# A hybrid SSD and attention layer: the projections of the next head are placed three steps ahead from the first step, and the lead shrinks by one step per head

## The chip, the core and the metric

One core of a Trainium2 chip runs the whole layer in one launch. The metric is the time of that launch in microseconds on the device. TensorE (PE) multiplies, VectorE (DVE), ScalarE (ACT) and GpSimd (POOL) do the element-wise work, SyncE (SP) issues most of the loads. Each engine works through its own instructions in the order in which they stand; semaphores make one engine wait for another.

## The reference

The layer normalises `x` (1024 tokens, 1024 wide), projects it once, and splits the columns between a Mamba-2 scan and a differential attention; both results go through an output projection, and a gated MLP follows. The change concerns the attention alone: 8 heads, each with two query and two key maps of 64 and a value of 128, queries and keys normalised and partly rotated, a mask by chunks of 64 keys.

```
q, k = rope(rms_norm(q)), rope(rms_norm(k))            # per head, 2 maps of 64
sc = einsum("bhjqd,bhjkd->bhjqk", q_blk, kt) * scale   # q_blk: 128 queries
p = softmax(where(mask, sc, -inf)); w = p[:, :, 0] - lam * p[:, :, 1]
o = einsum("bhqk,bhkv->bhqv", w, vt)
o = rms_norm(o, subln_w) * (1 - lambda_init)
```

## The kernel before

**Stages.** A start computes the normalised input, the whole projection of head 0 and the first three tiles of head 1. Then a loop of 64 steps runs the attention; step n is head h = n // 8 and place i = n % 8, which takes query tile `QORDER[i]` (0, 4, 1, 7, 2, 6, 3, 5; tile qt sees (qt + 1) x 128 keys). Scan, output projection and MLP follow; PE has little idle time there.

**One step.** The letters of `STEP = "SPWAB"` (line 37) are traced in this order: S, `softmax` of the next step's query tile (two score tiles `ps_s` in PSUM, one per map; DVE takes the maximum, ACT the exponential `pt`, DVE joins the two maps); P, `project`; W, `w_transpose` of this step's weights (`ps_wt` on PE, `wt` out on ACT or DVE); A, `values` of the step before (`po`; after each fourth tile `att_norm` squares the four results `ob` on ACT, and `att_store` transposes them, `ps_ot`); B, `build_qk` (`ps_qt` on PE, four casts `qka` on ACT, four subtractions on DVE, two copies on POOL).

**A projection tile.** `proj_mm(h, t)` is 24 matmuls of 384 columns (lines 209 to 211) into one `ps_pj`; `proj_post` (line 308) reads it with three ACT operations (`sq`, `raw`, `v`), two on DVE, and eight on POOL. `PROJ_AT[i]` (line 48) gives the tiles of head h + 1 that step i projects, `BUILD_AT[i]` those that it builds. Tiles 0 to 2 of head 1 were projected in the start, so steps 0 to 2 have none. Every head has one step with two tiles (place 5) and one with none (place 7); a step with no tile is called free below. When tile 7 is traced, the weights of the head after are loaded: `load_piece` casts the high part `wh` on ACT and subtracts on POOL or DVE. Two of the four pieces have a buffer for one head only, so their casts wait for the last matmuls of tile 7.

**What sets the order.** A scheduler lays the traced instructions out per engine and gives out the buffers; on the chip that order is fixed. PSUM has 3 slots `mm` (for `ps_pj`, `ps_qt`, `ps_wt`, `ps_ot`, `ps_tr`), 2 slots `s` (for `ps_s`, one per map, so one step's pair fills them) and one `o` (for `po`). A score matmul waits until the exponential of the map that held its slot is done.

Of the kernel before, what the change touches and what calls it, by code (L numbers as in the profile page):

```python
# [7 lines left out]
F32 = mybir.dt.float32  # L8
# [7 lines left out]
P = 128  # L16
S = 1024
NT = S // P
DK = 1024 // P
NH = 8  # L20
# [16 lines left out]
STEP = "SPWAB"  # L37
LAG = 1
WV = 1
RAW = 5  # L40
KT = 5
RS = 1

# [1 line left out]
START = "q0 w2 w3 q12 w1 q3 q4 q56 b0 b1 b3 w0 a0 a1 c1 c0 b2 b4 S0 p7 a2 r1 q7 b7 r0 c2 b5 b6 r2"  # L45
QORDER = [0, 4, 1, 7, 2, 6, 3, 5]

PROJ_AT = [[0], [1], [2], [3], [4], [5, 6], [7], []]
BUILD_AT = [[], [], [0], [1, 2], [3], [4], [5, 6], [7]]


PK_N1 = 0
# [22 lines left out]
def layer(ctx, tc, xT, wq0, wqkv, wxz, wout, wgu, wdn, pk, pb, cst, rot, sel, out):  # L75
# [137 lines left out]
    def proj_mm(h, t):  # L213
        ps = psa.tile([P, 512], F32, tag="mm", name="ps_pj")
        for k in KORDER:
            proj_k(h, t, k, ps)
        return ps
# [4 lines left out]
    ap_ = pool(actx, "att", side="right")  # L222
# [46 lines left out]
    for k in range(DK):  # L269
# [4 lines left out]
        n = 512 if k == 0 else S  # L274
# [22 lines left out]
    q0p = pool(a1ctx, "qk0")  # L297
# [10 lines left out]
    def proj_post(h, ts, pss_):  # L308
        hd = heads[h]
        n = len(ts)  # L310
        raws = []
        fac = ap_.tile([P, 2, 4], F32, tag="fac", name="fac", bufs=3)[:, :n]
        for i, (t, ps) in enumerate(zip(ts, pss_)):
            sq = a1.tile([P, 256], F32, tag="sq", name="sq", bufs=1)
            A.activation(sq, ps[:, 0:256], AF.Square)
            raw = a1.tile([P, 4, 64], F32, tag="raw", name="raw", bufs=RAW)
            raws.append(raw)
            q4 = raw.rearrange("p (i j) d -> p i j d", j=2)
            if h < WV:
                V.tensor_tensor(out=q4, in0=ps[:, 0:256].rearrange("p (i j d) -> p i j d", j=2, d=64), in1=b4(w_qk), op=ALU.mult)  # L320
            else:
                A.copy(out=raw.rearrange("p g d -> p (g d)"), in_=ps[:, 0:256])
                G.tensor_tensor(out=q4[:, :, :, 16:64], in0=q4[:, :, :, 16:64], in1=b4(w_qk[:, :, 16:64]), op=ALU.mult)
            v = (q0p, ap_)[h % 2].tile([P, P], F32, tag="v", name="v", bufs=8)
            A.activation(v, ps[:, 256:384], AF.Copy, scale=rtok[:, t : t + 1])
            hd["v"][t] = v
            if h == 0:
                V.tensor_scalar(out=dtt[:, t, :], in0=ps[:, 384:400], scalar1=rtok[:, t : t + 1], scalar2=None, op0=ALU.mult)
            V.tensor_reduce(out=fac[:, i], in_=sq.rearrange("p (g d) -> p g d", d=64), axis=AX.X, op=ALU.add)
            (V if h == 0 else G).tensor_scalar(out=fac[:, i], in0=fac[:, i], scalar1=1.0 / 64.0, scalar2=eps2[:, t : t + 1], op0=ALU.mult, op1=ALU.add)  # L330
            ta = a1.tile([P, 4, 16], F32, tag="ra", name="ra", bufs=2)
            tb = a1.tile([P, 4, 16], F32, tag="rb", name="rb", bufs=2)
            ta4 = ta.rearrange("p (i j) d -> p i j d", j=2)
            tb4 = tb.rearrange("p (i j) d -> p i j d", j=2)
            G.tensor_tensor(out=ta4, in0=q4[:, :, :, 0:16], in1=b4(cw[:, t]), op=ALU.mult)
            G.tensor_tensor(out=tb4[:, :, :, 0:8], in0=q4[:, :, :, 8:16], in1=b4(sw[:, t, :, 0:8]), op=ALU.mult)
            G.tensor_tensor(out=tb4[:, :, :, 8:16], in0=q4[:, :, :, 0:8], in1=b4(sw[:, t, :, 8:16]), op=ALU.mult)
            G.tensor_tensor(out=raw[:, :, 0:16], in0=ta, in1=tb, op=ALU.add)
        G.tensor_tensor(out=fac, in0=fac, in1=mhalf.unsqueeze(2).broadcast_to([P, n, 4]), op=ALU.pow)
        for i, t in enumerate(ts):  # L340
            V.tensor_tensor(out=raws[i], in0=raws[i], in1=fac[:, i].unsqueeze(2).broadcast_to([P, 4, 64]), op=ALU.mult)
            hd["qk"][t] = raws[i]
# [103 lines left out]
    class Piece:  # L446
        n = 0
# [121 lines left out]
    for op in START.split():  # L569
        t = int(op[1])  # L570
# [39 lines left out]

        return get

    def project(h, i):
        if h + 1 < NH:
            for t in PROJ_AT[i]:
                if h > 0 or t > 2:
                    proj_post(h + 1, [t], [proj_mm(h + 1, t)])
            if NT - 1 in PROJ_AT[i] and h + 2 < NH:
                for c in (2, 3, 0, 1):
                    load_piece(h + 2, c)  # L620
        else:
            half()
            if i == 2:
                dt_rates()
            if i == 4:
                dt_decays()
# [15 lines left out]
    for n, (h, i) in enumerate(steps):  # L642
        for part in STEP:
            if part == "S" and n + 1 < len(steps):
                h2, i2 = steps[n + 1]
                sm[n + 1] = softmax(h2, QORDER[i2])
            elif part == "P":
                project(h, i)
            elif part == "W":
                w, rl = sm.pop(n)  # L650
                todo[n] = (w, rl, w_transpose(QORDER[i], w))
            elif part == "B":
                for t in BUILD_AT[i]:
                    if h + 1 < NH:
                        build_qk(h + 1, t)
            elif part == "A":
                if n >= LAG:
                    values(n - LAG)
# [379 lines left out]
    for d in range(DK):  # L1038
        t = xq.tile([P, S], F32, name=f"x2_{d}")
# [443 lines left out]
```

## Time and profile before

| | |
|---|---|
| median of 3 runs | 1674.99 us (1673.95 to 1675.69) |
| profiled execution | 1673.81 us, its span 1672.0 us |
| PE busy | 1620.7 us, 97% of the span |
| DVE, ACT, POOL busy | 1138.0, 785.8, 776.2 us |
| the chain that ended last | PE 79%, DVE 9%, DMA 3%, ACT 3%, issue 3%, POOL 2% |
| step 0 begins, step 7 of head 0 begins | about 69 us, about 120 us |

Busy time of PE counts modelled ends of matmuls, so a busy PE need not be at its peak. In a timeline row the time in brackets is the idle time of the engine just before, with what ended it. From the first start to the next start of an instruction is what it takes in a row of work; a mean duration contains an overlap with the next.

### The profile page before, as it was taken

Reading aid. Unit: us, or ns where it says so; the run is one execution under the profiler, and the core shown is the slowest. Engines: PE = TensorE matmul, PEld = TensorE weight load, DVE = VectorE, ACT = ScalarE, POOL = GpSimd, SP = SyncE. Lnnn points to the kernel's source line nnn. Section 1 sums busy time; section 2 is a strip of 40 time slices with the busy share of each in tenths; the row PEclk is TensorE's granted clock in tenths of the full one; section 3 lists DMA queues with packets and bytes.
Section 4 is the critical chain, followed back from the end, with each engine's and each line's share of the span. In section 5 each row is a group of like instructions: output and inputs, shape, how many; then the busy total and the mean of one; then the engine's idle time right before and its main releaser. Section 6 shows DMA issues by size and latency. Waiting matters only on the chain.

```text
span 1672.0 us, 23812 instructions
## 1 busy us (share of the span) xinstructions
PE 1620.7 (97%) x8237; PEld 1378.3 (82%) x8237; DVE 1138.0 (68%) x2096; ACT 785.8 (47%) x1759; POOL 776.2 (46%) x975
## 2 busy tenths in 40 slices
PE   7899999999999999999999998899999999999998
PEld 7799999999988877877778876688888888777887
DVE  7778777777787667876752258855555555789877
ACT  5566675766666454445532234333333222534431
POOL 5856766675541232243324337733444443343225
PEclk9899999999999999999999999999999999999999
DMA  5101110110011110131325321432233222755523
GB/s 189 38 17 36 51 36 17 52 45 14 21 58 38 51 39 32 45 133 45 114 68 192 115 92 39 132 107 99 103 103 112 95 101 89 250 191 175 166 93 113
DMA packets 78135, 146.49 MB, mean 88 GB/s; under 512 B 8490, under 2 KB 16938, under 8 KB 78016
## 3 DMA queue, kind: packets, MB, share of 16 engines
q1 hardware_dynamic: 65216, 129.38, 23.1%
q0 software_dynamic: 2864, 10.10, 1.7%
q10 hardware_dynamic: 9936, 5.51, 1.1%
q8 instruction: 65, 1.06, 0.3%
q14 instruction: 54, 0.44, 0.1%
HBM read 110.09 MB, written 34.87 MB: 87 GB/s over the span
## 4 chain that ended last, share of the span: by engine, by line
PE 79%; DVE 9%; DMA 3%; ACT 3%; issue 3%; POOL 2%; SPq 0%; DVEq 0%; ACTq 0%; POOLq 0%
PE ps_pj L211 5%; PE ps_pj L209 5%; PE ps_pj L210 5%; PE ps_x L485 4%; PE ps_x L486 4%; PE ps_x L487 4%; PE ps_c L170 3%; PE ps_c L171 3%; PE ps_c L172 3%; PE ps_d L172 3%; PE ps_d L171 3%; PE ps_d L170 3%; PE ps_a L170 3%; PE p L172 3%; PE ps_a L171 3%; PE ps_a L172 3%
## 5 line engine op out<-in xcount | busy, mean ns | idle before, releaser
L158 ACT CAST op<-wr 128x512 fp32r<-128x512 f32 x156 | 96.2, 619 | 260.2 <-PE ps_d L172 77.7
L159 DVE TENSOR_TENSOR op<-wr,op 128x512 fp32r<-128x512 f32 x108 | 88.4, 820 | 146.4 <-ACT op L158 135.8
L1174 POOL TENSOR_TENSOR t<-wr,t 128x512 f32<-128x512 f32 (+2 forms) x72 | 93.6, 1299 | 193.9 <-issue 123.8
L209 PE MATMUL ps_pj<-wh,xwh 128*128 128x384 f32 (+1 forms) x512 | 175.7, 347 | 5.9 <-ACT wh L152 5.9
L211 PE MATMUL ps_pj<-wh,xwl 128*128 128x384 f32 (+1 forms) x512 | 174.0, 342 | 3.8 <-DVE xwl L278 3.8
L210 PE MATMUL ps_pj<-wl,xwh 128*128 128x384 f32 (+1 forms) x512 | 174.6, 342 | 0.0
L159 POOL TENSOR_TENSOR op<-wr,op 128x512 fp32r<-128x512 f32 x48 | 65.1, 1356 | 214.2 <-ACT op L158 213.9
L1174 POOL TENSOR_TENSOR t<-wr 128x512 f32<-128x512 f32 (+2 forms) x72 | 89.3, 1242 | 104.4 <-DVE op L159 33.6
L485 PE MATMUL ps_x<-xwh,op 128*128 128x512 f32 x320 | 130.3, 407 | 0.3 <-DVE raw L509 0.3
L486 PE MATMUL ps_x<-xwl,op 128*128 128x512 f32 x320 | 127.1, 397 | 0.0
L487 PE MATMUL ps_x<-xwh,op 128*128 128x512 f32 x320 | 127.1, 397 | 0.0
L382 ACT ACTIVATE pt<-ps_s,nm 128x640 f32<-128x640 f32 (+7 forms) x128 | 94.4, 740 | 47.3 <-DVE nm L377 20.0
L209 PEld LDWEIGHTS ps_pj<-wh,xwh 128*128 128x128 f32 x512 | 97.7, 191 | 6.5 <-ACT wh L152 5.9
L158 ACT CAST op<-t 128x512 fp32r<-128x512 f32 x80 | 49.5, 621 | 112.1 <-PE ps_c L172 55.6
L211 PEld LDWEIGHTS ps_pj<-wh,xwl 128*128 128x128 f32 x512 | 97.6, 191 | 4.9 <-DVE xwl L278 4.8
L171 PE MATMUL p<-y,op 128*128 128x512 f32 x256 | 100.8, 396 | 0.0
L172 PE MATMUL p<-y,op 128*128 128x512 f32 x256 | 100.6, 396 | 0.0
L170 PE MATMUL p<-y,op 128*128 128x512 f32 x256 | 99.0, 398 | 0.0
L159 DVE TENSOR_TENSOR op<-t,op 128x512 fp32r<-128x512 f32 x80 | 77.1, 966 | 32.0 <-ACT op L158 31.3
L210 PEld LDWEIGHTS ps_pj<-wl,xwh 128*128 128x128 f32 x512 | 97.7, 191 | 0.4
L377 DVE TENSOR_REDUCE nm<-ps_s 128x1 f32<-128x640 f32 (+7 forms) x128 | 94.0, 746 | 1.7
L410 PE MATMUL po<-v,wt 128*128 128x128 f32 x576 | 77.4, 276 | 0.3 <-DVE ob L420 0.3
(302 smaller groups left out, 4650.9 us busy)
## 6 DMA issues: line engine op xcount, KB each, us to landing
wr<-in_wgu_dram SPq DMA_DIRECT2D x88, 256.0 KB, 2.8
mr<-md SPq DMA_DIRECT2D x77, 256.0 KB, 3.7
wr<-in_wout_dram SPq DMA_DIRECT2D x48, 256.0 KB, 2.7
wr<-in_wqkv_dram SPq DMA_DIRECT2D x28, 384.0 KB, 3.1
wr<-in_wxz_dram SPq DMA_DIRECT2D x40, 256.0 KB, 2.8
wr<-in_wdn_dram SPq DMA_DIRECT2D x12, 768.0 KB, 4.8
md<-m SPq DMA_DIRECT2D x30, 256.0 KB, 2.0
big<-yd SPq DMA_DIRECT2D x10, 512.0 KB, 4.0
```

The costliest lines, as they stand in the source:

```text
L158: A.copy(out=op[:, 0:n], in_=src)
L159: eng.tensor_tensor(out=op[:, n : 2 * n], in0=src, in1=op[:, 0:n], op=ALU.subtract)
L170: T.matmul(out=ps, lhsT=wh, rhs=a[:, 0:512], start=first, stop=False, skip_group_check=more)
L171: T.matmul(out=ps, lhsT=wh, rhs=a[:, 512:1024], start=False, stop=False, skip_group_check=more)
L172: T.matmul(out=ps, lhsT=wl, rhs=a[:, 0:512], start=False, stop=last, skip_group_check=more)
L209: T.matmul(out=ps[:, :n], lhsT=xwh[k][:, ts], rhs=wh[:, k % 2, :], start=k == first, stop=False)
L210: T.matmul(out=ps[:, :n], lhsT=xwh[k][:, ts], rhs=wl[:, k % 2, :], start=False, stop=False)
L211: T.matmul(out=ps[:, :n], lhsT=xwl[k][:, ts], rhs=wh[:, k % 2, :], start=False, stop=k == last)
L485: T.matmul(out=ps, lhsT=wh[:, ks], rhs=xwh[k][:, fs], start=k == 0, stop=False)
L486: T.matmul(out=ps, lhsT=wh[:, ks], rhs=xwl[k][:, fs], start=False, stop=False)
L487: T.matmul(out=ps, lhsT=wl[:, ks], rhs=xwh[k][:, fs], start=False, stop=k == DK - 1)
L1174: G.tensor_tensor(out=self.t[name], in0=x, in1=y, op=ALU.subtract)
```

## The change

The two tables now hold, for each head, the step number n of each tile. Head 1: tiles 3 to 7 are projected in steps 0 to 4 (before in 3, 4, 5, 5, 6). Head 2: steps 6 to 13 (before 8 to 14, two of them in 13). Head 3: steps 15 to 22 (before 16 to 22, two of them in 21). Heads 4 to 7 keep their places. The builds follow: head 1 in steps 0 to 6, head 2 in 8 to 14, head 3 in 17 to 23. So the free steps up to step 23 are 5, 14 and 23 (before 0, 1, 2, 7, 15 and 23), and no step before 24 has two tiles. Six `raw` buffers (before 5) and 10 and 9 `v` buffers (before 8 each) hold what is made early; they cost memory alone.

```diff
-RAW = 5
+RAW = 6
...
-PROJ_AT = [[0], [1], [2], [3], [4], [5, 6], [7], []]
-BUILD_AT = [[], [], [0], [1, 2], [3], [4], [5, 6], [7]]
+PROJ_AT = {h: [9 * h - 12 + t for t in range(8)] if h < 4 else [8 * h - 8 + t - t // 6 for t in range(8)] for h in range(1, 8)}
+BUILD_AT = {h: [9 * h - 9 + (0, 1, 1, 2, 3, 4, 5, 6)[t] - (h > 1) for t in range(8)] if h < 4 else [8 * h - 8 + (2, 3, 3, 4, 5, 6, 6, 7)[t] for t in range(8)] for h in range(1, 8)}
+def at_step(table, n):
+    return [(h, t) for h, row in table.items() for t, m in enumerate(row) if m == n]
...
-            v = (q0p, ap_)[h % 2].tile([P, P], F32, tag="v", name="v", bufs=8)
+            v = (q0p, ap_)[h % 2].tile([P, P], F32, tag="v", name="v", bufs=(10, 9)[h % 2])
...
-    def project(h, i):
-        if h + 1 < NH:
-            for t in PROJ_AT[i]:
-                if h > 0 or t > 2:
-                    proj_post(h + 1, [t], [proj_mm(h + 1, t)])
-            if NT - 1 in PROJ_AT[i] and h + 2 < NH:
+    def project(n):
+        h, i = steps[n]
+        for h1, t in at_step(PROJ_AT, n):
+            proj_post(h1, [t], [proj_mm(h1, t)])
+            if t == NT - 1 and h1 + 1 < NH:
                 for c in (2, 3, 0, 1):
-                    load_piece(h + 2, c)
-        else:
+                    load_piece(h1 + 1, c)
+        if h == NH - 1:
             half()
...
-                project(h, i)
+                project(n)
...
-                for t in BUILD_AT[i]:
-                    if h + 1 < NH:
-                        build_qk(h + 1, t)
+                for h1, t in at_step(BUILD_AT, n):
+                    build_qk(h1, t)
```

On PE, at the start of the loop before (tiles numbered by the program: `ps_qt_797`, `_840` and `_853` build head 0; `ps_s_954` is a map of query tile 7; `ps_wt_909` and `ps_wt_939` are weights of steps 0 and 1):

```order
L350 MATMUL ps_qt_797<-cst_sb_60,raw_782 128x128 x2
L350 MATMUL ps_qt_840<-cst_sb_60,raw_550 128x128 x2
L372 MATMUL ps_s_954<-qka0_437 128x512
L373 MATMUL ps_s_954<-klo0_439,qka0_437 128x512
L350 MATMUL ps_qt_853<-cst_sb_60,raw_565 128x128 x2
L398 MATMUL ps_wt_909<-cst_sb_60,pt_712 128x128
L121 MATMUL ps_tr_914<-cst_sb_60,wide_67 40x128
L372 MATMUL ps_s_954<-qka0_437 128x512
L398 MATMUL ps_wt_939<-cst_sb_60,pt_898 128x128 x4
```

And now (`ps_s_1079` is the same map of query tile 7, `ps_pj_909` tile 3 of head 1, of which the first and last of 24 rows are shown, `ps_wt_952` the weights of step 0):

```order
L358 MATMUL ps_qt_797<-cst_sb_60,raw_782 128x128 x2
L358 MATMUL ps_qt_840<-cst_sb_60,raw_550 128x128 x2
L358 MATMUL ps_qt_853<-cst_sb_60,raw_565 128x128 x2
L380 MATMUL ps_s_1079<-qka0_437 128x512
L381 MATMUL ps_s_1079<-klo0_439,qka0_437 128x512
L217 MATMUL ps_pj_909<-wh_460,xwh4_102 128x384
...
L219 MATMUL ps_pj_909<-wh_506,xwl3_109 128x384
L406 MATMUL ps_wt_952<-cst_sb_60,pt_712 128x128
L358 MATMUL ps_qt_956<-cst_sb_60,raw_813 128x128 x2
L380 MATMUL ps_s_1079<-qka0_437 128x512
L381 MATMUL ps_s_1079<-klo0_439,qka0_437 128x512
L129 MATMUL ps_tr_970<-cst_sb_60,wide_67 40x128
```

A whole projection tile has come behind the first two scores of query tile 7, and the third build of head 0 ahead of them.

On PE, the free step at the end of head 0 before, from the last matmul of head 1's projections (`ps_pj_1386`) to the first of head 2's (`ps_pj_1568`); `ps_s_1495` and `_1496` are the maps of head 1's query tile 0, `ps_s_1545` and `_1546` those of tile 4:

```order
L211 MATMUL ps_pj_1386<-wh_506,xwl3_109 128x384
L398 MATMUL ps_wt_1453<-cst_sb_60,pt_1223 128x128 x4
...
L410 MATMUL po_1333<-v_567,wt_1331 128x128
L350 MATMUL ps_qt_1467<-cst_sb_60,raw_1262 128x128 x2
L372 MATMUL ps_s_1495<-qka1_438 128x128
...
L372 MATMUL ps_s_1496<-qka1_438 128x128
...
L350 MATMUL ps_qt_1480<-cst_sb_60,raw_1305 128x128 x2
L398 MATMUL ps_wt_1514<-cst_sb_60,pt_1375 128x128 x4
...
L372 MATMUL ps_s_1545<-qka1_438 128x512
...
L372 MATMUL ps_s_1546<-qka1_438 128x512
...
L350 MATMUL ps_qt_1530<-cst_sb_60,raw_1414 128x128 x2
L209 MATMUL ps_pj_1568<-wh_1430,xwh4_102 128x384
```

The stretch between the same two projections now, in step 5 (`ps_pj_1286` to `ps_pj_1479`); `ps_s_1395` is the second map of query tile 3, `ps_s_1456` and `_1457` those of tile 5, `ps_s_1551` the first map of head 1's tile 0, `ps_ot_1430` the first transposed result of head 0:

```order
L219 MATMUL ps_pj_1286<-wh_506,xwl3_109 128x384
L406 MATMUL ps_wt_1353<-cst_sb_60,pt_1178 128x128 x3
...
L418 MATMUL po_1049<-v_784,wt_1244 128x128
L358 MATMUL ps_qt_1379<-cst_sb_60,raw_1130 128x128 x2
L380 MATMUL ps_s_1395<-qka0_437 128x512
...
L380 MATMUL ps_s_1456<-qka0_437 128x512
...
L406 MATMUL ps_wt_1413<-cst_sb_60,pt_1275 128x128 x4
L406 MATMUL ps_wt_1420<-cst_sb_60,pt_1275 128x128 x3
L380 MATMUL ps_s_1457<-qka0_437 128x512
...
L380 MATMUL ps_s_1551<-qka1_438 128x128
...
L434 MATMUL ps_ot_1430<-cst_sb_60,ob_1368 128x128
...
L217 MATMUL ps_pj_1479<-wh_1330,xwh4_102 128x384
```

The free step has come from the narrow query tile 0 to the tiles 3 and 5, and less other work of PE stands in it.

On ACT, the same stretch before (`wh` casts of weights, `sq` and `v` of the last projection, `qka` casts of two builds, exponentials of query tile 0):

```order
L152 CAST wh_1442<-wr_1441 128x768
L315 ACTIVATE sq_1412<-ps_pj_1386 128x256
...
L325 ACTIVATE v_1417<-ps_pj_1386,rtok_73 128x128
L152 CAST wh_1448<-wr_1447 128x768
L401 COPY wt_1458<-ps_wt_1453 128x512
L352 CAST qka1_438<-ps_qt_1467 64x2x128
...
L352 CAST qka1_438<-ps_qt_1480 64x2x128
...
L382 ACTIVATE pt_1503,lt_1493<-ps_s_1495,nm_1494 128x128
L382 ACTIVATE pt_1507,lt_1493<-ps_s_1496,nm_1494 128x128
```

And now:

```order
L160 CAST wh_1342<-wr_1341 128x768
L323 ACTIVATE sq_1312<-ps_pj_1286 128x256
...
L333 ACTIVATE v_1317<-ps_pj_1286,rtok_73 128x128
L160 CAST wh_1348<-wr_1347 128x768
L409 COPY wt_1357<-ps_wt_1353 128x384
L424 ACTIVATE ob_1368,ss_1367<-po_1049,rl_718 128x128
...
L360 CAST qka1_438<-ps_qt_1379 64x2x128
...
L390 ACTIVATE pt_1406,lt_1392<-ps_s_1395,nm_1393 128x512
L409 COPY wt_1418<-ps_wt_1413 128x512
L160 CAST wh_2202<-wr_2201 128x768
L390 ACTIVATE pt_1468,lt_1454<-ps_s_1456,nm_1455 128x768
L160 CAST wh_2208<-wr_2207 128x768
```

The four squares `ob` (the first is shown) and two more weight casts (`wh_2202`, `wh_2208`) now stand ahead of or between the exponentials that free the slots of `ps_s_1395` and `ps_s_1456`.

## Rows read from the trace of the kernel before

**Rows 1.** Stretches: us, busy (count) of PE, PEld, DVE, ACT, POOL, clock, DMA share, GB/s.
```profile
70.00:75.00 5.00, 1.46 (x8) 0.89 (x6) 3.96 (x13) 2.72 (x7) 4.82 (x13) 0.99 0.00 0
75.00:85.00 10.00, 6.49 (x22) 4.86 (x23) 6.78 (x22) 5.59 (x18) 6.30 (x15) 0.50 0.00 0
85.00:86.00 1.00, 1.00 (x9) 0.96 (x8) 0.93 (x4) 0.00 (x0) 0.00 (x0) 0.93 0.00 0
210.00:270.00 60.00, 58.99 (x386) 57.03 (x385) 44.85 (x121) 40.94 (x122) 39.30 (x78) 1.00 0.12 36
```

**Rows 2.** Timeline of PE where head 0 starts: start us, us, instruction, idle before.
```profile
76.24 1.11 PE L350 MATMUL ps_qt<-cst_sb,raw 128*128 128x128 f32 x4 [2.33 <-DVE raw L341]
...
78.62 0.79 PE L372 MATMUL ps_s<-qka 128*128 128x512 f32 x1 [1.27 <-DVE qka L357]
...
81.48 0.37 PE L121 MATMUL ps_tr<-cst_sb,wide 128*40 128x128 f32 x1 [1.01 <-DVE klo L358]
```

**Rows 3.** Waits of PE from 92 to 480: us in total, times, longest.
```profile
PE ps_wt L398 <- ACT qka L355: 5.3, 7, 0.8
...
PE ps_qt L350 <- DVE raw L341: 1.2, 6, 0.2
```

**Rows 4.** Timeline of PE, the end of head 0.
```profile
113.38 0.47 PE L372 MATMUL ps_s<-qka 128*128 128x512 f32 x1
...
114.38 0.28 PE L372 MATMUL ps_s<-qka 128*128 128x256 f32 x1
...
114.84 0.60 PE L426 MATMUL ps_ot<-cst_sb,ob 128*128 128x128 f32 x4
...
119.69 0.60 PE L398 MATMUL ps_wt<-cst_sb,pt 128*128 128x128 f32 x4
...
120.12 1.73 PE L410 MATMUL po<-v,wt 128*128 128x128 f32 x14
...
124.80 0.41 PE L398 MATMUL ps_wt<-cst_sb,pt 128*128 128x128 f32 x2 [0.76 <-ACT qka L355]
```

**Rows 5.** Timeline of ACT at the same place.
```profile
118.27 0.90 ACT L382 ACTIVATE pt<-ps_s,nm 128x768 f32<-128x768 f32 x1
...
119.16 0.83 ACT L152 CAST wh<-wr 128x768 fp32r<-128x768 f32 x1
...
119.89 0.38 ACT L315 ACTIVATE sq<-ps_pj 128x256 f32<-128x256 f32 x1
...
121.40 0.60 ACT L401 COPY wt<-ps_wt 128x512 f32<-128x512 f32 x1
...
122.11 0.37 ACT L352 CAST qka<-ps_qt 64x256 fp32r<-64x256 f32 x1
...
123.43 0.37 ACT L352 CAST qka<-ps_qt 64x256 fp32r<-64x256 f32 x1
...
125.44 0.58 ACT L401 COPY wt<-ps_wt 128x512 f32<-128x512 f32 x1
...
125.91 0.85 ACT L152 CAST wh<-wr 128x768 fp32r<-128x768 f32 x1
...
128.51 0.36 ACT L416 ACTIVATE ob<-po,rl 128x128 f32<-128x128 f32 x1
...
129.88 0.36 ACT L352 CAST qka<-ps_qt 64x256 fp32r<-64x256 f32 x1
```

**Rows 6.** ACT from 92 to 480, by form: line, op, shapes, count | busy, mean ns.
```profile
L382 ACT ACTIVATE pt<-ps_s,nm 128x512 f32<-128x512 f32 x14 | 9.5, 685 | 1.5 <-DVE nm L377 1.3
```

**Rows 7.** DVE from 92 to 480, by form.
```profile
L358 DVE TENSOR_TENSOR klo<-ps_qt,qka 64x128 fp32r<-64x128 f32 x108 | 31.2, 289 | 1.5
...
L377 DVE TENSOR_REDUCE nm<-ps_s 128x1 f32<-128x768 f32 x14 | 12.3, 913 | 0.0
...
L388 DVE SCALAR_TENSOR_TENSOR pt<-pt,rat 128x512 f32<-128x512 f32 x7 | 7.7, 1096 | 0.2
...
L403 DVE COPY wt<-ps_wt 128x384 f32<-128x384 f32 x7 | 3.8, 548 | 0.0
```

## The prediction

> **What bounds the kernel now.** I read the windows by stretch first, since the page's shares are means over stages of different kinds. In the middle of the attention PE is busy 58.99 of 60 us at a granted clock of 1.00 (2.4 GHz), while DVE, ACT and POOL have 15 to 21 us to spare, and the DMA engines 0.88 of their time [rows 1]. So there a wait of PE is paid in full, and an engine that merely has more to do in a step costs nothing until it is late for PE. I then read PE's waits over the seven heads: they are nearly all at one place, 0.76 us for a cast `qka` in the free step that ends each head and 0.2 us for a `raw` in front of a build [rows 3]. Last I read the timeline where head 0 starts: PE waits 2.33, 1.27 and 1.01 us one after another, and over 75 to 85 it is busy only 6.49 of 10 us, all of it at a clock of 0.50 (1.2 GHz) [rows 1, 2].
>
> PE's work is the same before and after (the same matmuls, in another order), and behind the attention PE has little idle time in which a shift could vanish. So the change is worth the change in PE's waits plus that in the time it spends at half clock.
>
> **The start gains about 1.6 us.** The first projection tile of the loop (`ps_pj_909`) now stands behind the first two scores of query tile 7, which start at 78.62 [rows 2]. It stands behind the waits of 2.33 and 1.27 us, not ahead of them, so both stay. What it covers is the third, 1.01 us at 81.48. The tile's 24 matmuls, at 58.99 / 386 = 0.15 us each and twice that at half clock, give DVE 4 to 7 us to finish what PE waited for. I take the whole 1.01.
>
> The rest is clock. In 75 to 85 the 6.49 busy us ran at half rate; 1.11 + 1.03 us of them (the four `ps_qt`, and the scores from 78.62 to 79.65) lie ahead of the new tile and keep it. The other 4.35 would take 2.2 us at full clock. Before, the clock was back at 85 (0.93 in the slice from 85 to 86), 3.5 us after the last gap closed at 81.48 [rows 1, 2]. Now PE has no gap from 78.62 on, so by the same 3.5 us the clock is back at about 82.1, and 79.65 to 82.1 costs 1.2 us instead of 2.2. If it comes back only at 85 again, those 5.35 us cost 2.7 and the clock loses 0.5. So the start is worth 2.0 us at best, 0.5 at worst, and I take 1.6, near the row with the closed gap.
>
> **Three head ends go: 2.9 us gained.** Steps 7, 15 and 23 were free, each with 0.76 + 0.2 = 0.97 us of waits [rows 3]. Steps 7 and 15 now have a tile; 23 is free still and is priced anew below. Heads 4 to 7 keep their order and their waits.
>
> **Step 5 costs about 4.7 us.** This is the free step that decides. T is the end of tile 7 of head 1 on PE (`ps_pj_1286`). What PE has to do up to the next projection is 3 `ps_wt` (0.32 us, at 0.43 for four), 8 `po` (0.90, at 1.57 for 14), 2 `ps_qt` (0.22), the second map of tile 3 (0.50, half of what the four 512-wide matmuls before 114.38 take), the first map of tile 5 (0.73, half of 1.46), 7 `ps_wt` (0.75) [rows 4]: 3.42 us. Then it wants a score slot for `ps_s_1457`. There are two, and this one is freed by the exponential of `ps_s_1395`.
>
> ACT reaches that exponential after a row of work in program order [rows 5, 6]: 0.20 from PE's end to the first reading, 1.51 for `sq`, `raw`, `v` and the weight cast between them, 0.47 for `wt`, 1.37 for four `ob`, 1.32 for four `qka`, 0.69 for the exponential itself. That is T + 5.56, against PE's 3.42: **2.14 us of waiting**. The map takes 0.73 to T + 6.29. The next map (`ps_s_1551`) needs the slot of `ps_s_1456`, whose exponential stands behind another `wt` (0.47) and weight cast (0.73) and takes 0.89: T + 7.65, a wait of **1.36 us**. PE is then at T + 7.87 and wants `ob` for `ps_ot`. DVE can scale `ob` only after ACT's squares, at T + 3.55; it has two maxima of tile 5 (0.913 each), a `wt` (0.548), four build subtractions (0.289 each) and the join (1.096) ahead of that [rows 7], which makes T + 8.18, and with five small operations in between up to T + 9.4. That is a third wait, 0.3 to 1.5 us; I take 1.2, since DVE does nothing else in that stretch that could be dropped. Sum 4.7 us, with 3.8 to 5.0 by these ends. If ACT has the squares done earlier, as `po` ends early, nothing changes, since ACT works in order.
>
> Below that: if ACT were in fact as early as at the head ends of before, where the same casts and builds cost PE 0.97 us, step 5 would cost 0.97. That is the lower bound of this term, and a rival below.
>
> **Steps 14 and 23 cost about 2.1 and 2.0 us.** The same addition, from [rows 4 to 7]. In step 14 the first slot is freed by the exponential of a 128-wide map (`ps_s_2320`), on ACT behind 0.20 + 1.51 + 0.47, the copy `ya` (0.6, taken as a `wt`), a 768-wide exponential (0.89) and four `qka` (1.32); itself at 0.4 it ends at 5.4, and with the small steps of DVE ahead of these exponentials I take T + 5.8. PE has 17 transposes (two of them `ps_qt`) and 10 `po` at 0.11 and some 1.2 to 1.4 of scores: 4.35. That is 1.45, and 0.15 for the hand-over. The next slot comes at 7.4 (`wt`, weight cast and a narrow exponential later), PE is there at 6.85: 0.5. In step 23 the chain is 0.20 + 1.51 + 0.47 + 1.32 + 0.4 = 3.9, PE has 2.65: 1.25. Then a 640-wide map takes 0.62, its maximum and its exponential 0.8 each, with 0.4 between them: 6.6, against 5.8 for PE: 0.8. Lower bound again 0.97 each.
>
> **What costs nothing.** Each moved tile takes its 24 matmuls, three ACT, two DVE and eight POOL operations along; they leave the steps with two tiles, and those steps show no wait of PE, so nothing is won there. The loads of head 2's weights are issued two steps earlier on SP, in the same order against the other loads; at a DMA share of 0.12 [rows 1] they land in time. The added buffers are memory alone. If POOL's subtractions for the low parts of the new weights came late, the next tile would stop at its first low-part matmul; they are ready at about T + 6 and the tile starts after T + 9.
>
> **Sum.** +4.7 + 2.1 + 2.0 - 2.9 - 1.6 = **+4.3 us**. The profiled execution took 1673.81 us, so 1678.1; the median of the runs is 1674.99, 1.2 above it, and on that level the forecast is **1679.3 us**. With the bounds (start 0.5 to 2.0, step 5 3.8 to 5.0, the others half a us less or more) the case by itself reaches 1677 to 1681.5.
>
> **Rivals.**
> - *The clock falls in step 5, slower still.* From T + 3.4 to 9.1 PE has about 1 us of work in 5.7. The stretch 70 to 75, with 1.46 us of work in 5.00, is what preceded the fall to 1.2 GHz at the start [rows 1]. Against it: the start's gaps went on beyond 75. If it falls, the work until it returns runs at half rate: 3.5 us of it lose 1.75, ten us as in 75 to 85 lose 5. I take 2.7, nearer the low end since PE has work again from T + 9: 1682. The Trainium skill ("TensorE: Matmul & The Clock Gate", section "What's actually happening") has it that the throttled clock is the default and that activity releases it; the trace agrees, with 0.50 behind the idle stretch and 0.93 once the gaps were closed.
> - *Not slower: the waits of step 5 don't form.* ACT and DVE may run ahead of PE, so that the row of work isn't in one piece behind T, and each free step costs 0.97 as before. Then the free steps cancel, and the start remains: -1.6, 1673.4. It decides as soon as the three free steps together cost less than 2.9 + 1.6 = 4.5 us, against 8.8 in my sum. For it: ACT is busy only 40.94 of 60 us. Against it: the first link of the chain is the reading of `ps_pj_1286` itself, which can't come before T, and all that follows is on ACT in order.
> - *Faster: even steps close gaps that the trace hides.* PE's busy time has modelled ends; PEld shows 57.03 of 60 us where PE shows 58.99 [rows 1]. If those 2 us in 60 are waits in the steps with two tiles or none, spreading the tiles over three heads (some 60 us each) could give up to 6 us; half of that, 3 us on top of the last rival, makes 1670.4. Against it: no wait is named at those steps [rows 3]. The Trainium skill ("Perfetto Trace Analysis", section "Identifying the Most-Contended Engine") warns in this sense that the matmul busy share is a poor measure and the weight loads the better one; by the one PE has 1.0 us of 60 to give, by the other 3.0.
> - That the change doesn't do what it says is excluded by the order of the instructions, where each tile stands in its new step.
>
> **How the numbers follow.** Forecast 0.45, clock falls 0.17, waits don't form 0.27, hidden gaps 0.11. About 0.2% (3.3 us, 1671.6 to 1678.3) is what a measurement of this kernel can tell from no change. Of the forecast's 0.45 about 0.13 lie under 1678.3; of the second rival nearly all is inside, of the third 0.08 below. So faster 0.11, same 0.40, slower 0.49. The range is 1671.5 to 1684: it leaves out about half of the third rival and the upper part of the first.
>
> **What would show it.** Right: in step 5 PE idles about 4.7 us between `ps_pj_1286` and `ps_pj_1479`, ended by two exponentials and by `ob`; the waits at 124.80 and its like at the end of head 1 are gone; PE has no wait from 78.62 on, and the clock is at 1.00 by 82 to 85 and in step 5. Wrong: a clock of 0.50 behind step 5 (first rival), waits of 1 us there (second), or the same work of PE done in less time per head between 130 and 220 with no wait named (third).

## The result, and the profile after

The changed kernel took 1683.57 us (median of 4 runs, 1681.59 to 1686.66), the kernel before 1674.47: a ratio of 1.0054, 95% interval 1.0039 to 1.0070. Two more sets (experiments 1 and 12) gave 1.0050 (1.0038 to 1.0063) and 1.0052 (1.0037 to 1.0068). So it is slower by 8 to 9 us, where +4.3 was forecast; the time of 1683.57 lies inside the range, at its upper end, and the medians of the other two sets, 1684.46 and 1684.41, lie just above it. The direction is that of the forecast, and the amount is about twice it. The case by itself was put at 1677 to 1681.5, so the time is in the range only because the range makes room for the first rival.

The profiled execution of the changed kernel took 1681.59 us, its span 1679.8. Its timeline of PE, in the columns of [rows 2], gives the waits at the start, in steps 5, 14 and 23, and the first one that is left at a head end:

```profile
75.11 1.54 PE L358 MATMUL ps_qt<-cst_sb,raw 128*128 128x128 f32 x6 [2.02 <-DVE raw L349]
...
77.51 0.79 PE L380 MATMUL ps_s<-qka 128*128 128x512 f32 x1 [0.85 <-DVE qka L365]
...
85.80 0.29 PE L129 MATMUL ps_tr<-cst_sb,wide 128*40 128x128 f32 x1 [0.26 <-ACT v L333]
...
116.94 0.50 PE L380 MATMUL ps_s<-qka 128*128 128x512 f32 x1 [1.42 <-ACT pt L390]
...
119.04 0.33 PE L380 MATMUL ps_s<-qka 128*128 128x128 f32 x1 [1.14 <-ACT pt L390]
...
120.68 0.45 PE L434 MATMUL ps_ot<-cst_sb,ob 128*128 128x128 f32 x1 [1.20 <-DVE ob L428]
...
181.38 0.41 PE L358 MATMUL ps_qt<-cst_sb,raw 128*128 128x128 f32 x2 [1.15 <-POOL fac L338]
...
184.83 0.50 PE L380 MATMUL ps_s<-qka 128*128 128x512 f32 x1 [0.86 <-ACT pt L390]
...
186.93 0.50 PE L380 MATMUL ps_s<-qka 128*128 128x512 f32 x1 [0.26 <-ACT pt L390]
...
244.88 0.50 PE L380 MATMUL ps_s<-qka 128*128 128x512 f32 x1 [0.31 <-ACT pt L390]
...
248.25 0.38 PE L380 MATMUL ps_s<-qka 128*128 128x256 f32 x1 [0.44 <-ACT pt L390]
...
250.50 0.44 PE L358 MATMUL ps_qt<-cst_sb,raw 128*128 128x128 f32 x2 [1.75 <-DVE raw L349]
...
305.24 0.41 PE L406 MATMUL ps_wt<-cst_sb,pt 128*128 128x128 f32 x2 [0.76 <-ACT qka L363]
```

The three waits of 2.33, 1.27 and 1.01 us [rows 2] are now 2.02, 0.85 and 0.26. In step 5 PE waits for an exponential, for another, and for `ob`, 3.76 us in all. Step 14 has 2.27 us and step 23 has 2.50, but their longest waits stand at `ps_qt`, for `fac` and `raw`. The waits of 0.76 us at the ends of heads 0 to 2 [rows 3, 4] are gone; the like of them at 305.24 is the end of head 3, 4.58 us later than in the trace of before.

The windows of the same trace, in the columns of [rows 1], show the clock:

```profile
72.00:76.00 4.00, 1.69 (x6) 1.39 (x7) 3.51 (x11) 0.96 (x5) 3.82 (x10) 0.52 0.00 0
76.00:82.00 6.00, 5.15 (x17) 4.24 (x16) 3.96 (x14) 3.60 (x12) 3.64 (x10) 0.50 0.00 0
82.00:83.00 1.00, 1.00 (x6) 1.00 (x5) 0.00 (x0) 0.00 (x0) 0.00 (x0) 0.80 0.00 0
118.00:120.00 2.00, 0.44 (x2) 0.30 (x2) 1.97 (x5) 0.99 (x3) 1.94 (x3) 0.99 0.64 190
120.00:123.00 3.00, 2.32 (x9) 2.35 (x10) 3.00 (x7) 2.38 (x6) 2.48 (x3) 0.50 0.01 4
```

At the start it fell a little earlier than before, and was back at 82 to 83, where before it came back at 85 [rows 1]; but PE now had 5.15 us of work in the six from 76 to 82, all at half rate. From 120 to 123 there is a second stretch at 1.2 GHz, behind the waits of step 5. That is the first rival. Here and below, the loss of a stretch is the sum, over slices of 1 us, of PE's busy time times what the clock lacks to 1.00: 3.31 us before and 3.56 now at the start, and 1.34 behind step 5.

From the first wait in the loop (72.43 before, 71.31 now) to the `po` that waits at the end of the attention (489.35 before, 493.93 now), the loop takes 416.92 us before and 422.62 now: **+5.7**. Up to the loop the execution was 1.1 us shorter, with a shorter stretch at half clock around 34 to 45 (a loss of 3.4 instead of 5.1); in the two later traces of the changed kernel that loss is 5.0 and 5.1, so it belongs to the execution and not to the change. Behind that `po` stand the same instructions in the same order on every engine; they took 1182.65 us before and 1185.87 now: **+3.2**. The sum, -1.1 + 5.7 + 3.2, is the 7.8 us between the spans.

### The profile page after: what moved, and what is told of

The parts are those of the page before. It is cut to its first block, busy times and chain, and to the rows that moved or that the text cites. A ratio compares the mean times of both kernels' runs of the same rounds, so it can differ in the third digit from the quotient of the medians.

```text
span 1679.8 us, 23819 instructions
## 1 busy us (share of the span) xinstructions
PE 1623.3 (97%) x8237; PEld 1379.7 (82%) x8237; DVE 1141.6 (68%) x2096; ACT 787.0 (47%) x1759; POOL 769.6 (46%) x975
## 4 chain that ended last, share of the span: by engine, by line
PE 79%; DVE 10%; issue 3%; DMA 3%; ACT 2%; POOL 2%; SPq 0%; DVEq 0%; ACTq 0%; POOLq 0%
PE ps_pj L217 5%; PE ps_pj L219 5%; PE ps_pj L218 5%; PE ps_x L493 4%; PE ps_x L494 4%; PE ps_x L495 4%; PE po L418 3%; PE ps_c L178 3%; PE ps_c L179 3%; PE ps_c L180 3%; PE ps_d L178 3%; PE ps_d L179 3%; PE ps_d L180 3%; PE p L180 3%; PE p L178 3%
## 5 line engine op out<-in xcount | busy, mean ns | idle before, releaser
L380 PE MATMUL ps_s<-qka 128*128 128x512 f32 (+2 forms) x192 | 71.7, 379 | 8.1 <-ACT pt L390 7.1
```

## The experiments

Each result below starts with the ratio to the kernel before, run in the same set, and its 95% interval. "In the loop" is what the trace has more than the 416.92 us of before; "behind it" is the time from that `po` to the end, 1182.65 us before. Kernels with changed tables have the added buffers as well, unless it says otherwise.

**1. The changed kernel again.** No edit.

> The changed kernel once more, for the size. Its profile shows waits of 8.5 us in steps 5, 14 and 23 (3.76, 2.27, 2.50), 1.6 us fewer waits at the start and 2.9 fewer at head ends, so +4.0 us of waits up to step 24, one stretch at half clock behind step 5 (1.3 us), and another 3.2 us behind the attention, where the instructions are the same. Theory A (the 3.2 us belong to this one execution): ratio to the kernel before 1.003 to 1.0035. Theory B (the stages behind lose as well, in every execution): 1.005 to 1.006. The waits of steps 5, 14 and 23 should be the same to 0.1 us.

Ratio 1.0050. Its trace has the same waits to 0.1 us in steps 5, 14 and 23 (3.76, 2.36, 2.50), a loss of 1.51 behind step 5, +6.45 in the loop, and 1186.85 behind it. So the excess behind the attention is not a matter of one execution: theory A falls.

**2. A shift by 24 matmuls.** In `proj_mm` of the kernel before:

```
-        for k in KORDER:
-            proj_k(h, t, k, ps)
+        for _ in range(2 if (h, t) == (5, 3) else 1):
+            for k in KORDER:
+                proj_k(h, t, k, ps)
```

> The kernel before, with the 24 matmuls of tile 3 of head 5 done twice (the second pass starts the sum again, so the values stay): everything behind is only later by 24 x 0.174 = 4.2 us, the same kind of shift as the change makes. Theory A (a shift is worth itself): +4.2 us, ratio 1.0025, and the stages behind the attention as long as before. Theory B (the stages behind lose when they come some us later): +7 us or more, 1.004, with the excess behind the attention.

1.0025 (1.0012 to 1.0037), +4.24 in the loop, 1182.64 behind it. So a shift of this size is worth itself, and theory B falls as a general rule.

**3. One tile early.** The tables of before for heads 2 to 7, and for head 1:

```
+PROJ_AT[1] = [-1, -1, -1, 0, 3, 4, 5, 6]
```

> Of the change only the start: tile 3 of head 1 in step 0, tiles 4 to 7 in steps 3 to 6 one by one, free steps 1, 2, 7; heads 2 to 7 as before. By the sum of the prediction the start gains 1.6 us (1.0 of waits, 0.6 of clock) and no wide free step arises: -1.6 us, ratio 0.999. Rival (the start's gain is lost to another wait): 0. Rival (even steps close hidden gaps): head 1 takes over 3 us less.

1.0001 (0.9991 to 1.0010), and +0.06 in the loop, where the buffers alone have -1.6 (experiment 5). The wait of 1.01 goes here as well, but PE waits at other places instead:

```profile
85.61 0.77 PE L406 MATMUL ps_wt<-cst_sb,pt 128*128 128x128 f32 x5 [0.37 <-ACT v L333]
...
114.34 0.44 PE L217 MATMUL ps_pj<-wh,xwh 128*128 128x384 f32 x1 [0.54 <-DVE wt L411]
...
121.02 0.66 PE L406 MATMUL ps_wt<-cst_sb,pt 128*128 128x128 f32 x4 [0.24 <-ACT wt L409]
...
123.53 0.41 PE L406 MATMUL ps_wt<-cst_sb,pt 128*128 128x128 f32 x2 [0.97 <-ACT qka L363]
```

The first is at the start, the others are in the steps that lost their second tile and at the head end, and with the 0.28 that follows the last they are 1.2 us longer than the 1.24 that stood there before; the waits ahead of them at the start are 1.6 us shorter in sum, and half clock there costs 0.3 more. The rival is right: the gain is lost to other waits. Nothing is seen of a gain by even steps either.

**4. Builds out of step 5.** Head 1's row of the build table in the changed kernel:

```
-(0, 1, 1, 2, 3, 4, 5, 6)
+(0, 1, 1, 2, 3, 5, 6, 7)
```

> The changed kernel, with the builds of head 1's tiles 5, 6 and 7 one step later (steps 5, 6, 7). That takes four casts (1.32 us) off ACT ahead of the exponentials that free the score slots in step 5, and four subtractions (1.16 us) off DVE ahead of ob. Theory (ACT's row of work sets these waits): the waits of step 5 fall from 3.76 to about 2.5 us, steps 14 and 23 stay, the kernel is 1.2 us faster than the changed one (1.0047 against the kernel before). Rival (the weights' casts or the transfer of the weights set them): they stay at 3.7 us.

1.0049 (1.0036 to 1.0062); the waits of step 5 are 0.91, 1.28 and 1.59, in all 3.78. The theory failed, and the rival's number is what came; a further wait of 0.86 us now stands ahead of a projection at 131.06. The timeline of PE, then of ACT and of DVE in this kernel, shows why:

```profile
115.83 0.50 PE L380 MATMUL ps_s<-qka 128*128 128x512 f32 x1 [0.91 <-ACT pt L390]
...
118.08 0.33 PE L380 MATMUL ps_s<-qka 128*128 128x128 f32 x1 [1.28 <-ACT pt L390]
...
120.10 0.47 PE L434 MATMUL ps_ot<-cst_sb,ob 128*128 128x128 f32 x1 [1.59 <-DVE ob L428]
```

```profile
116.30 0.83 ACT L160 CAST wh<-wr 128x768 fp32r<-128x768 f32 x1 [0.53 <-DMA wr<-in_wqkv_dram]
...
117.04 0.90 ACT L390 ACTIVATE pt<-ps_s,nm 128x768 f32<-128x768 f32 x1
```

```profile
119.64 1.37 DVE L428 TENSOR_SCALAR ob<-po,rl,ss 128x128 f32<-128x128 f32 x4 [0.44 <-POOL ss L426]
```

With the casts gone ACT is earlier at the first exponential, though by less than 1.32 us, as a copy `wt` (0.58) has moved ahead of it; then it waits 0.53 us for the transfer of a weight, ahead of the second exponential. DVE is earlier, and waits 0.44 us for POOL's `ss`. Three chains (ACT's row, the weights, POOL and DVE) end within about half a microsecond of each other, and taking work off one brings up the next.

**5. The buffers alone.**

```
-RAW = 5
+RAW = 6
-v = ....tile([P, P], F32, tag="v", name="v", bufs=8)
+v = ....tile([P, P], F32, tag="v", name="v", bufs=(10, 9)[h % 2])
```

> The kernel before with nothing but the added buffers (6 raw, 10 and 9 v). The prediction called them memory alone: 0 us, ratio 1.000 (0.999 to 1.001). But the order shows that the sixth raw buffer lets the third build of head 0 come ahead of the scores of query tile 7, so at the start the waits of 2.33 and 1.27 may become 2.0 and 0.85 as in the changed kernel: up to 0.7 us less. Rival (the buffers move what lies behind the attention, and that is the excess of the changed kernel there): +2 to +3 us behind the attention, 1.0015.

0.9981 (0.9972 to 0.9990), -1.6 in the loop, 1184.76 behind it. "Memory alone" was wrong: with one more `raw` buffer the scheduler puts the third build of head 0 ahead of the scores of query tile 7. PE's timeline in this kernel (the first row holds six `ps_qt`, where [rows 2] have four):

```profile
75.02 1.54 PE L350 MATMUL ps_qt<-cst_sb,raw 128*128 128x128 f32 x6 [2.02 <-DVE raw L341]
...
77.42 0.79 PE L372 MATMUL ps_s<-qka 128*128 128x512 f32 x1 [0.85 <-DVE qka L357]
...
79.45 0.79 PE L372 MATMUL ps_s<-qka 128*128 128x512 f32 x1 [0.54 <-ACT qka L354]
```

So 0.85 and 0.54, for 1.27 and 1.01, come from the buffer and not from the tables. The 2.02 does not: over the twelve traces with the sixth buffer this wait is 2.02 to 2.32 us, and in the three of the changed kernel 2.02, 2.31 and 2.31. It is 2.02 to 2.09 where the clock fell before the scores ahead of this wait were done, and 2.31 or 2.32 where it fell later. Behind the attention this trace is 2.1 us longer than that of before, as the rival has it, but the runs are not longer and experiment 9 has 1182.5 there; so the runs speak against the buffers as what costs the changed kernel its excess, and do not settle it.

**6. Filling step 5.** In the changed kernel, `w_transpose` got a count `reps`:

```
-            for k in range(k0, k1):
+            for k in list(range(k0, k1)) * reps:
...
-                todo[n] = (w, rl, w_transpose(QORDER[i], w))
+                todo[n] = (w, rl, w_transpose(QORDER[i], w, 3 if n == 5 else 1))
```

> The changed kernel with the 7 transposes ps_wt of step 5 done three times (14 more matmuls, 1.5 us, same values), which stand on PE right ahead of its first wait of step 5. Theory: the wait of 1.42 us is filled, the other two (1.14 and 1.20) keep their ends, as ACT and DVE set them, so nothing is later; and with PE busier there the clock stays at 1.00 behind step 5, which saves 1.4 us: 1.0042 against the kernel before. Rival (the fall is not a matter of this idle time): the clock falls to 0.50 all the same, no change against the changed kernel, 1.005. Rival (the copies of the transposes come later and with them all): up to +1.5 us.

1.0052 (1.0040 to 1.0064). Timeline and windows of PE in step 5:

```profile
114.64 2.46 PE L406 MATMUL ps_wt<-cst_sb,pt 128*128 128x128 f32 x21
...
119.20 0.33 PE L380 MATMUL ps_s<-qka 128*128 128x128 f32 x1 [1.25 <-ACT pt L390]
...
121.00 0.47 PE L434 MATMUL ps_ot<-cst_sb,ob 128*128 128x128 f32 x1 [1.37 <-DVE ob L428]
```

```profile
116.00:120.00 4.00, 2.38 (x17) 1.82 (x14) 3.48 (x12) 3.12 (x7) 3.88 (x6) 1.00 0.38 126
120.00:124.00 4.00, 3.00 (x11) 3.00 (x12) 3.75 (x11) 3.32 (x9) 2.11 (x2) 0.57 0.20 45
```

The wait of 1.42 is filled, and the other two keep their ends within 0.6 us, as the theory has it. But the clock falls from 120 on all the same, so filling the first wait doesn't hold it: the first rival of this run is right, with the other two waits (1.25 and 1.37) still there.

**7. The store one step later.** In `values` of the changed kernel:

```
-        if "late" in todo:
+        if "late" in todo and n != 4:
```

> The changed kernel with the transposes ps_ot of head 0's first four results (and their store) one step later, in step 6 instead of 5; in the order the first scores of head 1's tile 0 then also come behind the projection. Theory (step 5's end is set by one chain that ends with ob on DVE, and the scores and ps_ot wait for it in a row): the waits of 1.14 and 1.20 us go, 1.42 stays, the clock holds at 1.00 behind step 5: 2.3 + 1.4 = 3.7 us less than the changed kernel, 1.0028 against the kernel before. Rival (the next po, which needs the slot that ob reads, or the projection's weights wait in their place): the same 3.8 us of waits in step 5 and 6, 1.005.

1.0018 (1.0010 to 1.0027): the only edit of the changed kernel that takes most of its loss away, 5 to 6 us. PE's timeline and windows:

```profile
116.87 0.50 PE L380 MATMUL ps_s<-qka 128*128 128x512 f32 x1 [1.42 <-ACT pt L390]
...
125.19 0.60 PE L434 MATMUL ps_ot<-cst_sb,ob 128*128 128x128 f32 x4
```

```profile
118.00:122.00 4.00, 4.00 (x25) 4.00 (x24) 3.92 (x11) 3.65 (x9) 3.80 (x5) 1.00 0.34 98
246.00:250.00 4.00, 3.14 (x11) 3.14 (x12) 3.86 (x10) 3.27 (x9) 1.53 (x2) 0.57 0.31 98
```

In step 5 the 1.42 us alone is left; the projection follows it without a gap, `ps_ot` comes at 125.19 without a wait, and the clock stays at 1.00 there. This execution had a fall behind step 23 instead (246 to 250, a loss of 1.4), where the executions of the changed kernel had none. The gain is larger than the 3.7 us expected, and the trace shows only a part of it where the theory has it: the loop is at +3.7, 2.0 us below the first trace of the changed kernel, and the part behind the attention took 1181.89 us, 4.0 below. So the waits of step 5 are shown to go, but not that they are worth 5 to 6 us.

**8. Head 1 alone.** The changed row for head 1, heads 2 and 3 as before (head 2 in steps 8 to 14, two tiles in 13).

> The changed tables for head 1 alone (projected in steps 0 to 4, steps 5, 6 and 7 free), heads 2 and 3 as before. By the traces: start -1.2 us (waits 1.6 less, clock 0.3 more), step 5 3.8 of waits and 1.4 of clock, the 0.97 at the end of head 0 gone, as nothing of a projection is left on ACT there: +3.0 us, ratio 1.0018, so that steps 14 and 23 make up the rest of the changed kernel's loss. Rival (three free steps in a row leave PE waiting in each): +6 us or more.

1.0006 (0.9997 to 1.0015). Step 5 has the same 1.42, 1.13 and 1.20, steps 6 and 7 none, and the 0.97 at the end of head 0 is gone; the trace gives +4.15 in the loop, with a longer stretch at half clock behind step 5 (a loss of 3.1). The waits are 1.3 us more than before. So neither number fits the expectation well: the loop of this trace is above it, and the time 2 us below. The profiled run, 1678.90 us, is near the top of the twelve (1674.60 to 1678.97), so what the waits of step 5 cost in most runs isn't settled by it.

**9. The sixth `raw` buffer alone.** `RAW = 6` in the kernel before, nothing else. The order on PE and ACT is that of experiment 5.

> The kernel before with the sixth raw buffer alone (v stays at 8). The order on PE and ACT is that of the kernel with all added buffers, which took 3.2 us less than the kernel before, 1.6 of them between its first wait in the loop and its end. Theory (the sixth raw buffer, by the third build that it lets come early, is the gain): the same waits of 2.02, 0.85 and 0.54 at the start, ratio 0.998 to 0.999. Rival (the v buffers or chance): 1.000.

0.9997 (0.9987 to 1.0006), with the waits of 2.02, 0.85 and 0.54. The waits of 0.85 and 0.54 are the buffer's, as expected; the gain in time isn't confirmed: the stretch at half clock at the start cost 5.0 us here against 3.3 in experiment 5, and the loop took 416.93 us, as before.

**10. The last build of each head one step later.** The tables and buffers of experiment 5, with

```
+BUILD_AT = {h: [8 * h - 8 + (2, 3, 3, 4, 5, 6, 6, 8)[t] for t in range(8)] for h in range(1, 8)}
```

> The tables of the kernel before, the added buffers, and the build of each next head's tile 7 one step later (step 0 of that head, which has a projection, instead of the free step 7). Theory (in a free step PE waits because ACT's row, here the four casts qka, is longer than PE's work): the 0.76 us at each of seven head ends goes, -5 us against the buffers alone, ratio 0.995. Rival (another wait takes its place, as when builds were moved out of step 5): 0.998 as with the buffers alone.

1.0000 (0.9991 to 1.0010), which neither the theory nor the rival has. The 0.2 us waits at the head ends go, and the 0.76 stays at each of them. PE and ACT there:

```profile
124.11 0.41 PE L406 MATMUL ps_wt<-cst_sb,pt 128*128 128x128 f32 x2 [0.76 <-ACT qka L363]
```

```profile
121.41 0.37 ACT L360 CAST qka<-ps_qt 64x256 fp32r<-64x256 f32 x1
...
123.76 0.26 ACT L363 CAST qka<-ps_qt 64x128 fp32r<-64x128 f32 x1
```

The free step still holds the eight casts of the two builds traced in step 6, and these were what PE waited for; the edit moved the one build that came later.

**11. Heads 1 and 2.** The changed rows for both, head 3 as before.

> The changed tables for heads 1 and 2 (free steps 5, 14 and 15), head 3 as before. Head 1 alone gave +4.2 us in the trace of the loop and 1.0006 in time. By the traces step 14 adds 2.3 us of waits, and the 0.97 at the end of head 1 goes: +1.3 against head 1 alone, ratio 1.0014. Rival (moving heads 2 and 3 costs more than their waits show, as 1.0006 against 1.005 hints): +4 us against head 1 alone, 1.003.

1.0040 (1.0027 to 1.0052), so about 5.7 us more than head 1 alone. The waits in the loop are 2.7 us more, not 1.3: step 14 has its 2.27, and in the free step behind it a new wait stands ahead of head 3's first projection, which neither head 1 alone nor the changed kernel has:

```profile
190.80 0.44 PE L220 MATMUL ps_pj<-wh,xwh 128*128 128x384 f32 x1 [1.16 <-DVE wt L414]
```

Behind the attention this execution took 1185.5 us against 1183.5 for head 1 alone. The rival is nearer.

**12. The changed kernel, third set.** No edit.

> The changed kernel a third time, beside the others. The loop takes 5.7 to 6.5 us more in its two traces, the runs gave 8.4 and 9.1. If the loop is all, 1.0035 to 1.004; if the excess is there in every set, 1.005. In the trace: waits of steps 5, 14 and 23 at 3.76, 2.3 and 2.5 again, and the clock at 0.50 behind step 5 again (if that is a matter of the waits and not of the execution); falls behind steps 14 or 23 in this trace would be a part of the excess.

1.0052 (1.0037 to 1.0068). The waits of steps 5, 14 and 23 are 3.75, 2.34 and 2.49, the loss behind step 5 is 1.54, the loop has +6.6, and 1186.4 us lie behind it. There is no fall behind steps 14 or 23. So the excess behind the attention is there in every set, and so is the fall behind step 5.

## Why the prediction came out as it did

By its terms, in us, with the three executions of the changed kernel (profile, experiments 1 and 12) against the profile of before:

| term | forecast | measured |
|---|---|---|
| start, waits | -1.0 | -1.6, -1.2, -1.2 |
| start, clock | -0.6 | +0.3, +0.4, +0.5 |
| head ends | -2.9 | -2.9 |
| step 5 | +4.7 | +3.8, +3.8, +3.8 |
| steps 14 and 23 | +4.1 | +4.8, +4.9, +4.8 |
| clock behind step 5 | 0 | +1.3, +1.5, +1.5 |
| the loop | +4.3 | +5.7, +6.5, +6.6 |
| behind the attention | 0 | +3.2, +4.2, +3.8 |

**Right.** The waits. That the free step moves to wide query tiles, and that ACT's row, then `ob` on DVE, hold PE there, is what the trace shows at 116.94, 119.04 and 120.68. The rows of PE, ACT and DVE that answer to the sum worked out from [rows 4 to 7]:

```profile
111.43 1.95 PE L418 MATMUL po<-v,wt 128*128 128x128 f32 x16
```

```profile
116.11 0.69 ACT L390 ACTIVATE pt<-ps_s,nm 128x512 f32<-128x512 f32 x1
...
117.99 0.91 ACT L390 ACTIVATE pt<-ps_s,nm 128x768 f32<-128x768 f32 x1
```

```profile
118.26 0.96 DVE L385 TENSOR_REDUCE nm<-ps_s 128x1 f32<-128x768 f32 x1
...
119.47 0.74 DVE L396 SCALAR_TENSOR_TENSOR pt<-pt,rat 128x512 f32<-128x512 f32 x1
...
120.13 1.36 DVE L428 TENSOR_SCALAR ob<-po,rl,ss 128x128 f32<-128x128 f32 x4
```

The first exponential ends at 116.8 and the second at 118.9; PE goes on 0.1 us behind each. `ob` stands at the end of a row of DVE that has no gap from 114.14 on, behind the maximum of the map that the first wait held up, and the join. The three waits were put at 2.14, 1.36 and 1.2 and are 1.42, 1.14 and 1.20. The first was mis-sized by a slip on PE's side of the sum: the 14 rows of `po` in [rows 4] are the seven matmuls of query tile 6, two rows each, so the eight `po` of query tile 7 are 16 rows, 1.78 us to the next start and not 0.90. With that the sum's own terms give 1.26. The second rival (the waits don't form) is out: the three free steps cost 8.5 us, not under 4.5.

**Steps 14 and 23: the size right by luck.** The sum held exponentials alone, with the same slip in step 14 (10 `po`, which are 20 rows). The waits for exponentials are 1.9 us in both steps together, where 4.1 was forecast. The other 2.9 us, 1.15 of step 14 and 1.75 of step 23, are builds (`ps_qt`) that wait for the last projected tile to pass through POOL and DVE, a chain that the sum left out. In step 23 most of it is one operation of DVE, beside a weight's subtraction on POOL:

```profile
248.78 1.67 DVE L349 TENSOR_TENSOR raw<-raw,fac 128x256 f32<-128x256 f32 x1
```

```profile
248.36 1.80 POOL L161 TENSOR_TENSOR wl<-wr,wh 128x768 fp32r<-128x768 f32 x1
```

The other 63 of these operations in this trace take 0.63 us at most, and this one takes 1.66 to 1.68 in all six traces with this step 23.

**Not so: the weights land in time.** In step 5 a cast on ACT waits for the transfer of its weight, where the prediction put no wait:

```profile
120.58 0.83 ACT L160 CAST wh<-wr 128x768 fp32r<-128x768 f32 x1 [1.60 <-DMA wr<-in_wqkv_dram]
```

It costs PE nothing here, as the projection has begun; in experiment 4 such a wait came ahead of an exponential.

**Failed: "the rest is clock", a gain of 0.6 at the start.** In the profiled execution the clock fell and came back 2 to 3 us earlier, so the stretch at half rate was as long as before, some 10 us; PE had more work in it, and over the three executions the loss grew by 0.3 to 0.5 us. Closing a gap was taken to shorten that stretch, and the work packed into it was not counted. That the clock was back at 82 to 83, near the forecast of 82.1, is luck: the last wait, from which the 3.5 us were to run, ended at 77.51 and not at 78.62.

**Failed: the clock behind step 5 at nothing.** The first rival is what happened, in all six traces that have the three waits (the changed kernel's three, experiments 4, 8 and 11) and in the one with the first of them filled. It cost 1.3 to 1.5 us, under its low end of 1.75, and 3.1 once; so the rival's total of 1682 came near the measured time partly by luck, as the excess behind the attention was in no rival. Experiment 7 has no fall there without the waits for the second exponential and for `ob`, in its one trace.

**Failed: "the change in PE's waits" as the whole account.** The step said that a shift passes through to the end. The instructions behind are the same, and yet took 3.2 to 4.2 us more. What is in the excess can be seen: before, they hold 20.6 us of waits and 6.8 of half-clock loss; in the three executions of the changed kernel 21.7 to 22.5, and 8.2 to 8.4, one stretch at half clock more; together that is 2.7 to 3.5 us of it. Laid beside the trace of before, matmul by matmul from that `po` on, the three traces run level with it up to about 825 us, are 1.5 to 1.6 us later behind the next stretch at half clock, and lose the other 1.7 to 2.6 us behind 1010 us. In that stretch the same gap ahead of the scan's `ps_y` (waits of 1.15 and 0.36 us), with the same 3.63 us of work in four, leaves the clock alone in the one kernel's trace and not in the other's. The windows around it, of before and then of the changed kernel:

```profile
824.00:828.00 4.00, 3.63 (x25) 2.79 (x25) 3.02 (x5) 0.00 (x0) 0.77 (x1) 1.00 0.18 66
```

```profile
829.00:833.00 4.00, 3.63 (x20) 2.90 (x20) 2.67 (x5) 0.00 (x0) 0.34 (x1) 0.62 0.21 66
```

Why is open. In thirteen traces, of all kernels but experiment 10 (which has no such `po` wait), the part behind takes 1182 to 1187 us. Ordered by when it begins:

| begins at (us) | takes (us) | kernel |
|---|---|---|
| 486.5, 488.1 | 1184.8, 1186.2 | experiments 5, 3 |
| 489.1, 489.4, 491.7, 493.2, 493.3 | 1182.5, 1182.7, 1181.9, 1183.5, 1182.6 | 9, before, 7, 8, 2 |
| 493.9, 494.1, 494.6, 494.7, 496.2, 496.3 | 1185.9, 1185.5, 1185.2, 1184.4, 1186.4, 1186.9 | changed, 11, 6, 4, 12, 1 |

Both the kernel before and kernels made from the changed one stand in the short group, so the tables and buffers alone don't decide it. That the time at which the part begins does is not shown: the order was found afterwards, and the fall behind `ps_y` doesn't follow it. It is there with beginnings at 489.1 and 493.9 (experiment 9, the changed kernel) and not with 489.4 and 494.1 (the kernel before, experiment 11). Experiment 2 shifted by 4.2 us, which lands in the short group; a shift by 6 or 7 us, which would test it, wasn't run.

The third rival (hidden gaps) is not seen anywhere: the terms of the table add up to the loop to 0.1 us, which leaves nothing for it, and experiment 3 had even steps in head 1 and gained nothing. By the weight-load share, which the Trainium skill ("Perfetto Trace Analysis", section "Identifying the Most-Contended Engine") prefers to the matmul busy share, there was something to gain; no run here shows it.

**No better version.** All the added buffers gave 0.9981 and the sixth `raw` buffer alone, with the same order on PE and ACT, 0.9997. Both are faster than the changed kernel, but that they beat the kernel before isn't settled.

## What to carry to other kernels

When a slack step is moved, work out what stands in it on every engine at the new place: here it left a step with 128-wide scores for one with 512 and 768, and what ACT and DVE took longer than PE's own work there was paid as waits of PE. When a row of a trace is used as a price, count whether its matmuls are those of the program: here one `po` is two rows. Where several chains end close together, taking work off one can bring up the next (experiment 4); placing later what PE asks for at that point took the waits away (experiment 7). And a buffer count is part of the order: a sixth buffer moved a build, with no line of the schedule changed.

## What the runs showed of the hardware

The waits for the second exponential and for `ob` at the end of step 5, 1.1 to 1.6 us each with some 0.4 us of work between them, were followed by a stretch at 1.2 GHz in each of the seven traces that have them; the single wait of 1.42 in experiment 7 was not. The waits of step 14 (1.15, 0.86 and 0.26 us in 5.5 us) were followed by none in seven traces, and those of step 23 by one in one of six (experiment 7). The pair of 1.15 and 0.36 us ahead of `ps_y` was followed by such a stretch in 9 of the 14 traces. The falls behind step 5 cost 1.3 to 1.5 us, and 3.1 once, so the 3.76 us of waits there cost 5.1 to 5.3 us in the three traces of the changed kernel.

An operation of DVE took four times as long beside one of POOL: `raw` of 128x256 took 1.62 to 1.68 us in the eight cases, over all traces, in which a `wl` of POOL ran beside it for 1.3 to 1.4 us, and 0.7 us at most everywhere else (0.42 as a rule). No run here was made to show the cause.
